# A fused decoder block on one core: low parts of 28 weight chunks are made early, kept in DRAM and loaded

## The chip, the core and the metric

The kernel runs on one core of a Trainium2 chip. Five engines each run their own instruction stream in order: TensorE (PE, matrix products into PSUM), VectorE (DVE), ScalarE (ACT), GpSimd (POOL) and SyncE (SP), which here only issues DMA transfers. GpSimd issues some transfers too. The metric is the time of one execution in device microseconds (us), the median of several runs. A run with the hardware profiler leaves a trace; its span, from the first to the last instruction, is a little shorter than the time.

## The reference

One decoder block on 512 tokens of width 1024, in fp32. The first half is token mixing: a combined input projection, a gated MLP with a causal position mixing, sliding-window attention with 16 heads, two gates, an output projection, and layer normalisation. The second half is a retrieval among 16384 single-neuron experts: each of 8 heads picks 16 experts for each token by a product of two key sets. Cut to what matters here:

```python
def peer_layer(xt, w_pq, sub_k1, sub_k2, peer_u, peer_v):
    ...
        v1, i1 = lax.top_k(s1, PEER_TOPK)
        v2, i2 = lax.top_k(s2, PEER_TOPK)
        ...
        sc, ci = lax.top_k(cand, PEER_TOPK)
        e = (...i1... * PEER_NKEYS + ...i2...)
        g = jax.nn.softmax(sc, axis=-1)
        act = gelu(jnp.einsum('thkd,td->thk', peer_u[e], xb))
        return jnp.einsum('thk,thkd->td', (g * act), peer_v[e])
```

peer_u and peer_v are matrices of 16384 rows of width 1024, called U and V below.

## The kernel before

**Split products.** A fp32 product is made as three products of a faster type: each operand is split into a high part (hi, a copy rounded by ScalarE) and a low part (lo = raw - hi, a subtraction). `mm3` (lines 62 to 64) adds hi\*hi, lo\*hi and hi\*lo in PSUM. For a chunk of weights, `load_split2` loads raw (128 x 1024, 512 KB) through SyncE's queue (L447), copies hi on ScalarE (L450) and subtracts lo, on VectorE (L458) or, in one stage, on GpSimd (L456). Four raw buffers, three hi and three lo are in turn.

**Dense experts.** For 384 of the 512 tokens the kernel doesn't gather rows: it multiplies all of them by all 16384 rows of U, in 128 chunks of 128 experts (psU, 24 matmuls of 128x384 a chunk), applies gelu, multiplies by the routing weights G and adds the products with V (acc). The last 128 tokens are done by gathers (ru, rv) that GpSimd issues, with VectorE doing the arithmetic.

**Stages.** In order of time: (1) modulation, projections and attention; 16 attention groups (4 blocks of queries x 4 groups of heads), each with its scores (pss), mask and softmax on VectorE and ScalarE (sm, ast), transposes of sm on TensorE (pt), a masked copy (pc, pp), and an output po that is split into oThi and oTlo; the products of w_gv are put between the groups to keep TensorE busy. Then w_u projections with a layer norm (vln), position mixing (pssp), gates and the output projection. (2) U chunks 3 and up beside the top-k, whose instructions a generator issues between chunks (`pump`). Their activations go to a DRAM tensor (Ad). (3) The spread: for 24 batches of 16 tokens, VectorE builds one-hot tiles oh (L633 to L637), TensorE multiplies them into a dense weight table (psg, L645 and L646), ScalarE copies that into stg (two buffers), and SyncE writes it to a DRAM tensor Gd (L658). Beside it run 28 more U chunks. Of the first 21 the activations stay in SBUF (`res`, the resident chunks; before: 32 to 52), and their part of the table is multiplied straight from stg, so it isn't written. (4) V products of the resident chunks, then U and V of the remaining ones in runs of up to 8 chunks (G is loaded from Gd by run), then V products of the spilled chunks, with Ad loaded back.

**What sets the order.** The program is written in the order in which the engines get it, with the generators' instructions put in by `pump`; a scheduler with priorities then orders each engine's stream. In SyncE's stream a transfer waits for its buffer, and all behind it wait too.

## Time and profile before

| | |
|---|---|
| time, median of 3 runs | 1730.35 us (1728.38 to 1731.13) |
| the profiled execution | 1727.13 us, span 1725.4 us |
| mean granted TensorE clock | 0.993 of full speed |
| TensorE busy | 1667.5 us, 97% of the span |
| VectorE busy | 1346.7 us, 78% |
| ScalarE busy | 685.6 us, 40% |
| GpSimd busy | 474.2 us, 27% |
| DMA | 409.52 MB, mean 237 GB/s |

A share of the whole span is a mean over stages with different limits, so the stages have to be read apart. TensorE's matmuls are pipelined and their ends are modelled: a busy TensorE is not one at its peak. An instruction is busy from its start; what it waited for stands as idle time before it.

### The profile page before, as it was taken

How to read it: one execution, taken by the hardware profiler on the slowest of the kernel's cores; microseconds unless marked ns; L12 is line 12 of the kernel's file. 1: busy time of each engine (PE TensorE's matmuls, PEld its weight loads, DVE VectorE, ACT ScalarE, POOL GpSimd, SP SyncE). 2: the span in 40 equal slices, each digit the busy share in tenths (PEclk: the TensorE clock that was granted, in tenths of full speed). 3: DMA queues.
4: the chain of work that ended last, by engine and by line, in shares of the span. 5: the costliest groups of instructions: out<-in, count | busy, mean ns of one | idle time of the engine just before them, and what ended most of it. 6: DMA issues, size and time to landing. Idle time of an engine off the chain costs nothing.

```text
span 1725.4 us, 23595 instructions
## 1 busy us (share of the span) xinstructions
PE 1667.5 (97%) x8658; PEld 1440.2 (83%) x8658; DVE 1346.7 (78%) x2510; ACT 685.6 (40%) x1095; POOL 474.2 (27%) x333
## 2 busy tenths in 40 slices
PE   6999999999999999999999999999999999999997
PEld 3865778788788999999987789999999999988776
DVE  6467785554559999999988887878787888787687
ACT  3467632233333333455443233333333333343333
POOL 2000000000043455300014544434444545541102
PEclk9999999999999999999999999999999999999999
DMA  7502267642232355566599999999899899899973
GB/s 270 200 1 74 98 198 256 210 144 95 86 120 85 112 173 174 209 218 226 203 316 365 373 328 333 325 339 348 306 336 334 326 336 341 303 372 312 306 235 106
DMA packets 158695, 409.52 MB, mean 237 GB/s; under 512 B 19217, under 2 KB 66097, under 8 KB 158322
## 3 DMA queue, kind: packets, MB, share of 16 engines
q1 hardware_dynamic: 121186, 273.47, 46.2%
q0 software_dynamic: 36960, 134.50, 21.6%
q8 instruction: 68, 1.11, 0.3%
q14 instruction: 49, 0.40, 0.1%
q10 hardware_dynamic: 432, 0.04, 0.0%
HBM read 376.88 MB, written 30.82 MB: 236 GB/s over the span
## 4 chain that ended last, share of the span: by engine, by line
PE 52%; DVE 20%; issue 5%; DMA 4%; POOL 2%; ACT 1%; SPq 0%; DVEq 0%; POOLq 0%; ACTq 0%
PE acc L802 7%; PE acc L803 7%; PE acc L799 7%; PE psU L64 6%; PE psU L62 6%; PE psU L63 6%; POOL ru L669 2%; DMA ar<-Ad 2%; DMA wa<-in_w_ada_dram 2%; DVE oh L634 1%; DVE loU L458 1%; DVE oh L637 1%; DVE oh L633 1%; DVE oh L636 1%; DVE loV L458 1%
## 5 line engine op out<-in xcount | busy, mean ns | idle before, releaser
L62 PE MATMUL psU<-h2Thi,hiU 128*128 128x384 f32 x1008 | 340.9, 338 | 5.4 <-ACT hiU L450 3.7
L64 PE MATMUL psU<-h2Thi,loU 128*128 128x384 f32 x1008 | 340.4, 338 | 3.5 <-DVE loU L458 3.4
L63 PE MATMUL psU<-h2Tlo,hiU 128*128 128x384 f32 x1008 | 339.2, 337 | 0.0
L802 PE MATMUL acc<-loV,wh 128*128 128x512 f32 x768 | 301.5, 393 | 5.5 <-DVE loV L458 5.5
L803 PE MATMUL acc<-hiV,wl 128*128 128x512 f32 x768 | 300.5, 391 | 0.3 <-DVE wl L785 0.3
L799 PE MATMUL acc<-hiV,wh 128*128 128x512 f32 x768 | 298.8, 389 | 1.7 <-ACT wh L784 1.7
L669 POOL DMA_INDIRECT ru<-in_peer_u_dram,idx x128 | 157.2, 1228 | 368.6 <-DVE ru L673 351.5
L682 POOL DMA_INDIRECT rv<-in_peer_v_dram,idx x128 | 174.1, 1360 | 248.3 <-DVE facc L688 221.4
L458 DVE TENSOR_TENSOR loV<-rawV,hiV 128x1024 fp32r<-128x1024 f32 x128 | 156.3, 1222 | 90.3 <-ACT hiV L450 90.2
L450 ACT ACTIVATE hiV<-rawV 128x1024 fp32r<-128x1024 f32 x128 | 135.1, 1056 | 224.3 <-PE psU L63 188.6
L450 ACT ACTIVATE hiU<-rawU 128x1024 fp32r<-128x1024 f32 x126 | 133.9, 1062 | 216.6 <-POOL loU L456 68.0
L62 PEld LDWEIGHTS psU<-h2Thi,hiU 128*128 128x128 f32 x1008 | 190.5, 189 | 8.8 <-ACT hiU L450 3.9
L64 PEld LDWEIGHTS psU<-h2Thi,loU 128*128 128x128 f32 x1008 | 190.3, 189 | 5.3 <-DVE loU L458 5.2
L63 PEld LDWEIGHTS psU<-h2Tlo,hiU 128*128 128x128 f32 x1008 | 190.6, 189 | 2.6
L802 PEld LDWEIGHTS acc<-loV,wh 128*128 128x128 f32 x768 | 144.1, 188 | 39.5 <-DVE loV L458 10.9
L673 DVE SCALAR_TENSOR_TENSOR ru<-ru,h2n 128x1024 f32<-128x1024 f32 x128 | 154.4, 1220 | 24.3 <-DMA ru<-in_peer_u_dram,idx 24.1
L803 PEld LDWEIGHTS acc<-hiV,wl 128*128 128x128 f32 x768 | 144.1, 188 | 30.8 <-DVE wl L785 1.0
L799 PEld LDWEIGHTS acc<-hiV,wh 128*128 128x128 f32 x768 | 144.2, 188 | 30.5 <-ACT wh L784 2.0
L688 DVE SCALAR_TENSOR_TENSOR facc<-rv,wg,facc 128x1024 f32<-128x1024 f32 x126 | 159.4, 1279 | 11.4 <-DMA rv<-in_peer_v_dram,idx 11.4
L784 ACT ACTIVATE wh<-wf 128x384 fp32r<-128x384 f32 x107 | 56.1, 525 | 182.1 <-DVE wf L780 106.2
L456 POOL TENSOR_TENSOR lopq<-rawpq,hipq 128x1024 fp32r<-128x1024 f32 x16 | 39.0, 2445 | 322.2 <-ACT hipq L450 322.2
L458 DVE TENSOR_TENSOR loU<-rawU,hiU 128x1024 fp32r<-128x1024 f32 x96 | 116.9, 1218 | 2.8 <-ACT hiU L450 2.8
(629 smaller groups left out, 2929.4 us busy)
## 6 DMA issues: line engine op xcount, KB each, us to landing
rawU<-in_uT_dram SPq DMA_DIRECT2D x128, 512.0 KB, 4.2
rawV<-in_peer_v_dram SPq DMA_DIRECT2D x128, 512.0 KB, 6.2
wa<-in_w_ada_dram SPq DMA_DIRECT2D x48, 512.0 KB, 4.2
G<-Gd SPq DMA_DIRECT2D x11, 1536.0 KB, 14.8
Gd<-stg SPq DMA_DIRECT2D x24, 600.0 KB, 4.3
rawpq<-in_w_pq_dram SPq DMA_DIRECT2D x16, 512.0 KB, 3.6
Ad<-act SPq DMA_DIRECT2D x39, 192.0 KB, 2.2
ar<-Ad SPq DMA_DIRECT2D x9, 768.0 KB, 8.5
```

The source lines that it names most:

```text
L62: nc.tensor.matmul(ps, l.hi, r.hi, start=(i == 0), stop=False)
L63: nc.tensor.matmul(ps, l.hi, r.lo, start=False, stop=False)
L64: last = nc.tensor.matmul(ps, l.lo, r.hi, start=False, stop=(i == n - 1))
L450: h = nc.scalar.activation(hi, raw, AF.Copy)
L458: last["dve"] = nc.vector.tensor_sub(lo, raw, hi.bitcast(F32))
L669: d = nc.gpsimd.indirect_dma_start(out=rows, out_offset=None, in_=I["peer_u"], in_offset=bass.IndirectOffsetOnAxis(ap=idx[:, s:s + 1], axi ...
L673: paced(nc.vector.scalar_tensor_tensor(rows, rows, 1.0, h2n, op0=ALU.mult, op1=ALU.mult, accum_out=wg[:, s:s + 1]))
L682: nc.gpsimd.indirect_dma_start(out=rows, out_offset=None, in_=I["peer_v"], in_offset=bass.IndirectOffsetOnAxis(ap=idx[:, s:s + 1], axis=0))
L688: paced(nc.vector.scalar_tensor_tensor(fa, rows, wg[:, s:s + 1], fa, op0=ALU.mult, op1=ALU.add))
L799: m = nc.tensor.matmul(acc, l.hi, r.hi, start=st, stop=False)
L802: nc.tensor.matmul(acc, l.hi, r.lo, start=False, stop=False)
L803: nc.tensor.matmul(acc, l.lo, r.hi, start=False, stop=sp_)
```

## The change

A generator `presplit` is added to the first stage. For each of the last 28 chunks of U (100 to 127) it loads raw (praw, two buffers) through GpSimd's queue, makes hi (phi) on ScalarE and lo (plo) on VectorE, one buffer each, and writes lo to a new DRAM tensor LoD, again through GpSimd's queue. It advances one step after each attention group (two after every fourth), one in each w_u projection, and what is left is issued behind the position mixing. Its loads are kept behind the second of two small transfers kd on that queue. The filling of sm with a constant, in the first four groups, goes from GpSimd to VectorE.

In the spread stage the chunks beside the spreading are now 100 to 127 (before 32 to 59), in the same number: 100 to 120 resident, 121 to 127 spilled. For them `load_split2` loads lo from LoD through SyncE in place of subtracting. Raw is loaded and hi is copied as before. The chunks that are run later with V are 32 to 99 (before 60 to 127). As the resident columns of the table stand elsewhere, the write of stg to Gd has other pieces: 128x1600 and 128x112 in place of 128x512 and 128x1200.

```diff
+NPS = 28
...
+    LoD = dram.tile([NPS, P, D], F32, name="LoD")
...
+        def presplit():
+            raws = {}
+
+            def load(k):
+                raws[k] = pre.tile([P, D], F32, name=f"praw{k}", tag="praw", bufs=2)
+                behind(nc.gpsimd.dma_start(raws[k], I["uT"][NCH - NPS + k]), kd_copy)
+            load(0)
+            for k in range(NPS):
+                if k + 1 < NPS:
+                    load(k + 1)
+                yield
+                hi = pre.tile([P, D], F32R, name=f"phi{k}", tag="phi", bufs=1)
+                lo = pre.tile([P, D], F32R, name=f"plo{k}", tag="plo", bufs=1)
+                nc.scalar.activation(hi, raws[k], AF.Copy)
+                nc.vector.tensor_sub(lo, raws[k], hi.bitcast(F32))
+                nc.gpsimd.dma_start(LoD[k], lo.bitcast(F32))
+        ps_steps = presplit()
...
             else:
-                nc.gpsimd.memset(sm, NEG)
+                nc.vector.memset(sm, NEG)
...
                 u = 4 * n + gh
+                for _ in range(2 if u % 4 == 3 else 1):
+                    next(ps_steps, None)
...
             ps = proj_T(load_split(I["w_u"][j], f"u{j}"), hT, f"psu{j}")
+            next(ps_steps, None)
...
             nc.vector.tensor_sub(aT.lo[:, g, :], mf, aT.hi[:, g, :].bitcast(F32))
+        for _ in ps_steps:
+            pass
         sp_.close()
+        pre_.close()
...
-    def load_split2(src, nm, pool=None):
+    def load_split2(src, nm, pool=None, low=None):
...
-        if last.get("pool"):
+        if low is not None:
+            nc.sync.dma_start(lo.bitcast(F32), low)
+        elif last.get("pool"):
             last["pool_lo"] = nc.gpsimd.tensor_sub(lo, raw, hi.bitcast(F32))
...
-        w = load_split2(I["uT"][i], f"U{i}")
+        w = load_split2(I["uT"][i], f"U{i}", low=LoD[i - NCH + NPS] if i >= NCH - NPS else None)
...
-        res["first"] = cur[0] + 1
+        res["first"] = NCH - NPS
...
-    i = NPRE + 1
+    todo, ready = list(range(NPRE + 1, NCH - NPS)), list(range(NCH - NPS, NCH))
     while not done or len(res["ids"]) < NRES:
-        cur[0] = i
+        i = (ready if res and ready else todo).pop(0)
...
     for _ in range(VDLY):
+        i = (ready or todo).pop(0)
         U_chunk(i, False)
...
-    uvruns = runs(range(i, NCH))
+    todo += ready
+    uvruns = runs(todo)
```

VectorE's stream where the attention groups begin, before. wloq and wwlogv are low parts of weights, sm0_0 and sm0_1 the scores of the first two groups.

```order
L120 TENSOR_TENSOR wloq7_493<-rawq7_490,whiq7_492 128x1024
L130 TENSOR_TENSOR wwlogv0_577<-rawwgv0_3_590,wwhigv0_576 128x1024
L254 COPY_PREDICATED sm0_0_543<-mcur_i_533,pss0_0_544 128x512
L258 TENSOR_REDUCE ast0_0_551<-sm0_0_543 128x4
L259 TENSOR_TENSOR ast0_0_551<-ast0_0_551,sink_538 128x4
L260 TENSOR_SCALAR ast0_0_551<-ast0_0_551 128x4
L261 TENSOR_TENSOR ast0_0_551<-sink_538,ast0_0_551 128x4
L254 COPY_PREDICATED sm0_1_594<-mcur_i_533,pss0_1_595 128x512
```

The same place now; a row with L224 is a subtraction of `presplit`.

```order
L127 TENSOR_TENSOR wloq7_497<-rawq7_494,whiq7_496 128x1024
L137 TENSOR_TENSOR wwlogv0_585<-rawwgv0_3_598,wwhigv0_584 128x1024
L224 TENSOR_TENSOR plo2_742<-praw2_640,phi2_741 128x1024
L224 TENSOR_TENSOR plo3_749<-praw3_706,phi3_748 128x1024
L283 COPY_PREDICATED sm0_0_547<-mcur_i_537,pss0_0_548 128x512
L287 TENSOR_REDUCE ast0_0_555<-sm0_0_547 128x4
L288 TENSOR_TENSOR ast0_0_555<-ast0_0_555,sink_542 128x4
L289 TENSOR_SCALAR ast0_0_555<-ast0_0_555 128x4
L290 TENSOR_TENSOR ast0_0_555<-sink_542,ast0_0_555 128x4
L283 COPY_PREDICATED sm0_1_602<-mcur_i_537,pss0_1_603 128x512
L287 TENSOR_REDUCE ast0_1_610<-sm0_1_602 128x4
L224 TENSOR_TENSOR plo4_819<-praw4_746,phi4_818 128x1024
```

Two subtractions, plo2 and plo3, stand between the last weights and the first masking (COPY_PREDICATED), and plo4 stands inside the second group's softmax.

GpSimd's stream behind the two kd transfers, now (before, two fillings of sm, MEMSET, and the masking of wst followed there).

```order
L236 DMA kd1_386<-kd1_386 64x512
L215 DMA praw0_580<-in_uT_dram 128x1024
L215 DMA praw1_582<-in_uT_dram 128x1024
L225 DMA LoD_79<-plo0_636 128x1024
L215 DMA praw2_640<-in_uT_dram 128x1024
L225 DMA LoD_79<-plo1_702 128x1024
L215 DMA praw3_706<-in_uT_dram 128x1024
L225 DMA LoD_79<-plo2_742 128x1024
```

Each load praw stands ahead of the store LoD of the chunk before; a store waits for its subtraction, and the next load waits behind it.

SyncE's stream in the middle of the spread, before: the writes of the table by batch (stg0_2 is batch 2 of the first 128 tokens), and the raw chunks.

```order
L658 DMA Gd_76<-stg0_2_6217 128x512
L658 DMA Gd_76<-stg0_2_6217 128x1200
L658 DMA Gd_76<-stg0_3_6304 128x512
L658 DMA Gd_76<-stg0_3_6304 128x1200
L447 DMA rawU41_6793<-in_uT_dram 128x1024
L658 DMA Gd_76<-stg0_4_6391 128x512
L658 DMA Gd_76<-stg0_4_6391 128x1200
L447 DMA rawU42_6880<-in_uT_dram 128x1024
```

Now:

```order
L690 DMA Gd_76<-stg0_2_6418 128x1600
L690 DMA Gd_76<-stg0_2_6418 128x112
L486 DMA loU106_6732<-LoD_79 128x1024
L690 DMA Gd_76<-stg0_3_6505 128x1600
L690 DMA Gd_76<-stg0_3_6505 128x112
L486 DMA loU107_6819<-LoD_79 128x1024
L477 DMA rawU110_7081<-in_uT_dram 128x1024
L690 DMA Gd_76<-stg0_4_6592 128x1600
```

A load loU stands between the writes of two batches, behind the write of an earlier one, and the loads rawU run four chunks ahead of it.

And SyncE's stream at the end of the spread, now.

```order
L690 DMA Gd_76<-stg2_6_8205 128x1600
L690 DMA Gd_76<-stg2_6_8205 128x112
L486 DMA loU125_8363<-LoD_79 128x1024
L750 DMA Ad_77<-act124_8287 128x384
L477 DMA rawU126_8396<-in_uT_dram 128x1024
L690 DMA Gd_76<-stg2_7_8290 128x1600
L690 DMA Gd_76<-stg2_7_8290 128x112
L486 DMA loU126_8399<-LoD_79 128x1024
L750 DMA Ad_77<-act125_8391 128x384
L477 DMA rawU127_8432<-in_uT_dram 128x1024
L486 DMA loU127_8435<-LoD_79 128x1024
L477 DMA rawV100_8468<-in_peer_v_dram 128x1024
```

Chunk 127's raw stands behind the write of chunk 125's activations (act125), and the loads of the last two low parts stand just ahead of and behind it.

## Rows read from the trace of the kernel before

**Rows 1.** The page, busy time, share of the span and instructions of each engine.

```profile
PE 1667.5 (97%) x8658; PEld 1440.2 (83%) x8658; DVE 1346.7 (78%) x2510; ACT 685.6 (40%) x1095; POOL 474.2 (27%) x333
```

**Rows 2.** Table by stages: length, busy us (instructions), granted clock, DMA share, GB/s.

```profile
84.00:196.00 112.00, 110.92 (x530) 70.96 (x530) 73.06 (x179) 75.32 (x207) 1.05 (x2) 1.00 0.09 29
196.00:231.00 35.00, 34.76 (x154) 28.42 (x153) 29.83 (x42) 21.12 (x25) 1.59 (x1) 1.00 0.64 218
231.00:260.00 29.00, 24.32 (x139) 20.76 (x137) 28.12 (x43) 11.65 (x16) 0.00 (x0) 0.98 0.57 192
...
713.00:890.00 177.00, 169.18 (x1443) 162.79 (x1444) 170.86 (x207) 91.43 (x180) 3.80 (x3) 0.97 0.68 236
890.00:1000.00 110.00, 102.91 (x456) 83.65 (x455) 90.04 (x134) 35.86 (x47) 54.03 (x44) 1.00 0.99 364
1000.00:1500.00 500.00, 500.00 (x2531) 455.38 (x2530) 403.22 (x499) 182.11 (x241) 229.33 (x174) 1.00 0.93 330
```

**Rows 3.** TensorE's timeline, 713 to 891 us: start, length, operation, idle before.

```profile
713.15 0.45 PE L617 MATMUL ptg<-ident,gs 128*128 128x128 f32 x1 [2.32 <-DVE gs L597]
...
723.96 0.24 PE L645 MATMUL psg<-oh,oh 128*128 128x128 f16 x1
...
725.76 0.22 PE L646 MATMUL psg<-oh,oh 128*128 128x128 f16 x1
...
882.68 0.33 PE L64 MATMUL psU<-h2Thi,loU 128*128 128x384 f32 x1
...
889.96 0.33 PE L64 MATMUL psU<-h2Thi,loU 128*128 128x384 f32 x1
890.14 0.39 PE L799 MATMUL acc<-hiV,wh 128*128 128x512 f32 x1
```

**Rows 4.** VectorE's groups, 713 to 890 us: count, busy us, mean ns, idle before.

```profile
L458 DVE TENSOR_TENSOR loU<-rawU,hiU 128x1024 fp32r<-128x1024 f32 x26 | 31.6, 1215 | 2.3 <-ACT hiU L450 2.3
L636 DVE TENSOR_TENSOR oh<-oh,gT 128x2048 f16<-128x2048 f16 x24 | 29.1, 1214 | 0.1
```

**Rows 5.** DMA issues of the whole run: count, KB each, median us to landing.

```profile
rawU<-in_uT_dram SPq DMA_DIRECT2D x128, 512.0 KB, 4.2
...
rawpq<-in_w_pq_dram SPq DMA_DIRECT2D x16, 512.0 KB, 3.6
Ad<-act SPq DMA_DIRECT2D x39, 192.0 KB, 2.2
...
ru<-in_peer_u_dram,idx POOLq DMA_INDIRECT x128, 7.4
```

**Rows 6.** Waits of SyncE's DMA queue, 700 to 930 us: total, times, longest.

```profile
SPq L447 <- DVE loU L458: 68.9, 21, 8.2
```

**Rows 7.** The page, costliest groups: count, busy us, mean ns, idle before.

```profile
L669 POOL DMA_INDIRECT ru<-in_peer_u_dram,idx x128 | 157.2, 1228 | 368.6 <-DVE ru L673 351.5
...
L450 ACT ACTIVATE hiU<-rawU 128x1024 fp32r<-128x1024 f32 x126 | 133.9, 1062 | 216.6 <-POOL loU L456 68.0
```

**Rows 8.** GpSimd's timeline, 30 to 90 us.

```profile
58.72 0.57 POOL L207 DMA_DIRECT2D kd<-kd  x1
```

**Rows 9.** DMA issues between 50 and 80 us.

```profile
kd<-kd POOLq DMA_DIRECT2D x2, 128.0 KB, 2.5
```

**Rows 10.** VectorE's timeline, 72 to 93 and 194 to 198 us.

```profile
84.40 0.73 DVE L254 COPY_PREDICATED sm<-mcur_i,pss 128x512 f32<-128x512 int32 x1 [7.84 <-PE pss L249]
...
196.08 0.43 DVE L288 TENSOR_TENSOR oTlo<-po,oThi 128x256 fp32r<-128x256 f32 x1 [0.43 <-ACT oThi L287]
```

**Rows 11.** TensorE's timeline, 81 to 93 us.

```profile
90.48 0.60 PE L271 MATMUL pt<-ident,sm 128*128 128x128 f32 x4
```

**Rows 12.** VectorE's groups, 84 to 196 us.

```profile
L274 DVE TENSOR_TENSOR pc<-pt,mcurT 128x512 f32<-128x512 f32 x16 | 11.0, 687 | 5.9 <-PE pt L271 5.8
...
L288 DVE TENSOR_TENSOR oTlo<-po,oThi 128x256 fp32r<-128x256 f32 x15 | 6.4, 423 | 14.8 <-ACT oThi L287 14.7
...
L259 DVE TENSOR_TENSOR ast<-ast,sink 128x4 f32<-128x4 f32 x16 | 2.5, 155 | 0.1
```

More of the change, by code (lines that the diff above doesn't have):

```diff
@@ L65, in mm3, with behind @@
         return last
+    def behind(ins, other):
+        tc.add_manual_dep(ins.ins, other.ins.name,
+                          mybir.DependencyInfo(mybir.DependencyClass.NoSync, mybir.DependencyReason.DATA))
     const = ctx.enter_context(tc.tile_pool(name="const", bufs=1, reuse_waits="tile"))
@@ L197, in block_kernel @@
                 nc.tensor.matmul(ps, w.lo[:, k, :], hT.hi[:, k, :], start=False, stop=(k == NK - 1))
+        pre_ = ExitStack()
+        pre = pre_.enter_context(tc.tile_pool(name="pre", bufs=1, reuse_waits="tile"))
+        def presplit():
[14 more added lines that the diff above has]
+        ps_steps = presplit()
         att = ExitStack()
@@ L206, in block_kernel @@
         nc.gpsimd.dma_start(kd[0][64:128, :], kd[0][0:64, :])
-        nc.gpsimd.dma_start(kd[1][0:64, :], kd[1][64:128, :])
+        kd_copy = nc.gpsimd.dma_start(kd[1][0:64, :], kd[1][64:128, :])
         vT = ap_.tile([P, S], F32, name="vT", tag="pc", bufs=2)
@@ L435, in block_kernel @@
     last = {}
-    def behind(ins, other):
-        tc.add_manual_dep(ins.ins, other.ins.name,
-                          mybir.DependencyInfo(mybir.DependencyClass.NoSync, mybir.DependencyReason.DATA))
     def paced(ins):
         behind(ins, last["dve"])
-    def load_split2(src, nm, pool=None):
+    def load_split2(src, nm, pool=None, low=None):
         raw = pw.tile([P, NK * P], F32, name=f"raw{nm}", tag="raw", bufs=4)
@@ L710, in U_chunk @@
     def U_chunk(i, keep_act):
-        w = load_split2(I["uT"][i], f"U{i}")
+        w = load_split2(I["uT"][i], f"U{i}", low=LoD[i - NCH + NPS] if i >= NCH - NPS else None)
         ps = pu.tile([P, SD], F32, name=f"psU{i}", tag="mm", bufs=2)
@@ L816, in block_kernel @@
     res = {}
-    cur = [NPRE]
     def end_topk():
@@ L867, in block_kernel @@
             pump(GPUMP if res else UPUMP + 1.2 * bool(last.get("pool")))
-        i += 1
     open_v()
     for _ in range(VDLY):
+        i = (ready or todo).pop(0)
         U_chunk(i, False)
@@ L873, in block_kernel @@
         pump(2.7)
-        i += 1
-    uvruns = runs(range(i, NCH))
+    todo += ready
+    uvruns = runs(todo)
     for n, j in enumerate(res["ids"]):
@@ L899, in block_kernel @@
     left = 260 - n_g
-    for run in runs(spilled):
+    for run in runs(sorted(spilled)):
         load_G(run)
```

## The prediction

> **What bounds the kernel now.** The share of busy time says TensorE, 97% of the span [rows 1]. That is an average, so I cut the span into stages [rows 2]. Three of them are touched.
>
> The spread stage runs from its first transpose at 713.15 to the first product with V at 890.14, 177.0 us [rows 3]. VectorE is busy 170.86 of the 177 there [rows 2], and the groups show with what: 24 batches, each with four builds of 1.21 us, and 26 subtractions loU of 1.215 us, 31.6 us together [rows 4]. TensorE's 169.18 looks nearly full, but its records overlap and stretch when it is fed late, so I count its own need from step lengths. psU matmuls follow each other every (889.96 - 882.68)/42 = 0.1733 us, psg matmuls every (725.76 - 723.96)/31 = 0.0581 us [rows 3]. By program order there are 668 psU and 768 psg matmuls between those two ends: 115.8 + 44.6 = 160.4 us. The 48 changes between the two shapes and the nine transposes have no row of their own; I put them at 3.6, a little above one psg step each: 164.0 (without them 160.4). So TensorE loses 13.0 us here, and that is the most that freeing VectorE can return; the 31.6 us are not.
>
> The attention stage, 84 to 196 us, is the opposite: TensorE 110.92 of 112.00, VectorE 73.06, ScalarE 75.32, DMA share 0.09 [rows 2]. Work put on VectorE has room, but a TensorE instruction that waits for it costs its full wait. In the next stage (196 to 231) VectorE has 29.83 of 35, and from 231 to 260 it is full, 28.12 of 29 [rows 2].
>
> The third is the entrance to V, 890 to 1000: DMA share 0.99, 364 GB/s, and TensorE 102.91 of 110 [rows 2]. There bytes are the price.
>
> **The spread.** 26 to 28 loU subtractions leave VectorE: 31.6 us, and up to 34. Its 170.86 falls to about 138 of 164, and TensorE's 164 becomes the bound. In their place come as many loads loU of 512 KB. In the order SyncE issues them behind the Gd write of an earlier batch, and their buffer (three) is free when TensorE has finished the chunk three before. I followed the order: most are asked for 12 to 15 us before use, and a load of 512 KB lands in 4.2 us [rows 5]. DMA: before, 236 GB/s x 177 us = 41.8 MB; 24 more loads are 12.6 MB, 54.4 MB in 164 us, 331 GB/s. From 1000 to 1500 DMA carries 330 GB/s at a share of 0.93 with TensorE at 500.00 of 500 [rows 2], so this is at the edge but carried. A wait that goes: rawU's buffer was freed by the subtraction, and SyncE waited 68.9 us in all for it [rows 6]; now ScalarE's copy frees it. Where it ends is less good. The last three chunks (125 to 127) have rawU and loU issued behind writes of act, with leads of 3.5 to 7.7 us against 4.2 of landing; VectorE would have needed 1.2 us there. I leave 3.5 us of TensorE's wait in place. Value 13.0 - 3.5 = **-9.5 us**; bounds 0 (every load as late as the subtraction was) and -13.0.
>
> The Gd writes change from 128x512 + 128x1200 to 128x1600 + 128x112, the same bytes, 448 B a row in the small one. Two staging buffers cover a batch of some 7 us each, and a write of 600 KB should land near rawU's 4.2 for 512 KB [rows 5]: nothing, unless it passes some 12 us.
>
> **The front.** 28 subtractions of 1.22 us and 28 copies on ScalarE of 1.06 us [rows 7] come here. In the attention stage 17 of them: VectorE 73 + 20.7 + four moved memsets, some 95 of 112; ScalarE 75 + 18 = 93 of 112. By busy time they fit. What may not fit is the wait. plo has one buffer: subtraction k+1 can't write before the store LoD of k has landed, and VectorE is in order, so everything behind it waits for that round trip r. No row shows a 512 KB store from POOL's queue. Its parts: the issue on POOL took 0.57 us for kd and 1.23 us for ru [rows 7, 8]; the landing of kd, 128 KB on that queue, 2.5 us, of Ad (192 KB, to DRAM) 2.2, of rawpq (512 KB) 3.6 [rows 5, 9]. From Ad to rawpq 320 KB cost 1.4 us, so 384 KB more than kd cost 1.7: 2.5 + 1.7 = 4.2, and I take r = **4.3** from the subtraction's end; bounds 3.6 (a landing like rawpq's, its issue hidden) and 7.4 (the median of the gathers ru on that queue [rows 5]).
>
> By program order plo2 and plo3 stand back to back ahead of the first masking. Before, VectorE idled 7.84 us until 84.40 [rows 10]; I put plo1's end at 74.2, plo2's at max(79, 78.5) + 1.2 = 80.2, plo3's at 80.2 + 4.3 + 1.2 = 85.7. The first masking begins 1.3 us late, and plo4 follows inside the second group: it starts at 85.7 + 4.3 = 90.0, after which the first group's sm is done at 92.9, where TensorE had used it at 90.48 [rows 11]: 2.4 us lost at once. Group four, with small pieces around its subtraction, I put at 1.6 more: **+4**.
>
> After that, between plo3 and plo19, the order has 16 pieces of VectorE work. With mean durations by shape (0.69, 0.42 and 0.16 us [rows 12], 1.22 for 128x1024) they are 3.3, 4.3, 3.5, 5.6, 3.4, 6.5, 2.7, 12.9, 4.1, 3.9, 4.4, 4.4, 4.2, 4.9, 4.2 and 4.2 us. A step is the larger of its piece and r, and 1.22. With r = 4.3 the sum is 81.7 + 19.5 = 101.2, plo19 ends at 186.9, and the last oTlo 4.9 us later at 191.8, ahead of the 196.08 of before [rows 10]. So only the early stalls stay. With r = 5.0 it is 90.0 + 19.5 from 86.4: 195.9, last oTlo 200.8, +4.7; beyond that each 0.1 us of r costs 1.3 us: +8.6 at 5.3, +11 at 5.5, +18 at 6. The front is thus **+4**, bounds +1 (r = 3.6) and, at 7.4, more than 30.
>
> Behind attention 11 subtractions are left for 196 to 260: 8 of them beside the w_u projections, where VectorE has 5 us free and gets 10 more of work, part of which moves into the full 29 us; it ends at a wait of TensorE that the +4 already contains if VectorE arrives early. I add nothing, and up to 3 for the range.
>
> DMA pays nothing here: 0.09 of it was used in attention, and 17 x 1.05 MB in 112 us are 160 GB/s.
>
> **A rule that speaks against it.** On POOL's queue the trace shows the ru issue at 1228 ns against 570 for kd [rows 7, 8], both beside a working VectorE. The Trainium skill, "SBUF — State Buffer", section "Who interferes with whom", says that descriptors of DMAs issued from GpSimd can't be written while VectorE runs a copy, cast or tensor_scalar in a two-port mode, and that tensor_tensor doesn't hinder it. In the attention stage nearly all of VectorE's work is tensor_tensor, reduce or masked copy, so by that rule r would stay as short as I take it; with the gap of 0.66 us between the two issues added to each trip r would be 5.0 and the front +4.7 or a little more. The same skill, "DMA: Bandwidth & Descriptors", section "Anatomy of one DMA — SWDGE (gpsimd) path", warns that the completion of a write into HBM can take surprisingly long; Ad's 2.2 us into DRAM [rows 5] doesn't show that on SyncE's queue, and no run here shows it on POOL's.
>
> **The entrance to V.** Three chunks' loU (125 to 127) fall on or next to the stage where DMA is full: 1.57 MB / 364 GB/s = 4.3 us if all of it delays the V loads; most of it is asked for before 890. Value **+1**, bounds 0 and +4.3. The chunks later read in runs are 32 to 99 instead of 60 to 127, 68 both times, the spilled ones 39 both times: nothing.
>
> **Sum.** -9.5 + 4 + 1 = -4.5 us. The profiled execution took 1727.13 us, 3.2 below the median of 1730.35; to that median the forecast is **1725.9 us**.
>
> **The rivals.** *A, the forecast*: spread -7 to -13, front +1 to +5: 1717 to 1726.8. *M, the front takes it back*: r of 5.0 to 5.4, front +5 to +10 and a little in the stages behind; with -9.5 and +1 the sum is -3.5 to +3.4, 1729 at its middle. For it: one buffer, 17 trips, and no slack in TensorE; against it: Ad's short landing. *B, slower, the LoD round trip*: the same place, but decided from r = 5.5 on, where the front's loss passes 12 us: r of 5.5 to 6 gives +3.5 to +10, 1734 to 1740. For it: the gathers' 7.4 on the same queue; against it: those are indirect. *C, slower, the loads pace the spread*: SyncE's one queue carries rawU, loU, Gd and Ad in order, a Gd write waits for ScalarE's stg, and a loU behind it is late; it decides when the lead of 12 to 15 us falls below the landing, which at 297 GB/s or more (331 asked) may grow. Then the stage keeps its 177 us and the front's +4 and the +1 remain: 1735. For it: the 0.99 share behind 890 with TensorE losing 7 us [rows 2]; against it: 1000 to 1500.
>
> **How the numbers follow.** About 0.2% (3.5 us) is what a measurement of this kernel can tell from no change. A 0.45, M 0.27, B 0.16, C 0.12. So faster 0.45, same 0.27, slower 0.28. The range takes A's better end and most of B and C: 1716 to 1739; A alone would be 1717 to 1727.
>
> **What would show it.** Right: loU gone from VectorE between 713 and 890, that stage near 167 us with VectorE near 140, no long TensorE wait for a loU load before chunk 125; in the front each plo waiting about a trip behind the one before, the first group's transposes of sm some 2 us later, the last oTlo before 197. Wrong: LoD landing above 5 us after its subtraction (then M or B, with VectorE's waits named LoD from 84 to 196 and the last oTlo past 200), or psU idle behind DMA loU in many chunks of the spread (C). If the spread gains more than 13 us, my step lengths are wrong.

## The result and the profile after

The changed kernel is slower: 1741.01 us median (1738.57 to 1743.42) against 1729.37 for the kernel before on the same chip, a ratio of 1.0066 with a 95% interval of 1.0049 to 1.0084. The profiled execution took 1740.37 us, span 1738.6, mean granted clock 0.987.

Busy times, the page's first part, for [rows 1]: VectorE has as much work as before, only elsewhere; ScalarE has 27 us more and GpSimd 34.

```profile
PE 1668.6 (96%) x8658; PEld 1439.3 (83%) x8658; DVE 1348.4 (78%) x2514; ACT 712.8 (41%) x1123; POOL 508.2 (29%) x385
```

The table by stages, for [rows 2], with the spread stage (727 to 897) and the entrance to V (897 to 1007) where they now lie; columns as there.

```profile
84.00:196.00 112.00, 105.30 (x512) 68.03 (x511) 86.57 (x191) 89.06 (x221) 17.03 (x32) 0.95 0.56 190
196.00:231.00 35.00, 30.34 (x124) 22.36 (x123) 29.09 (x41) 20.64 (x25) 6.45 (x11) 0.90 0.73 256
...
727.00:897.00 170.00, 166.18 (x1453) 160.20 (x1451) 142.93 (x180) 93.72 (x183) 4.55 (x4) 1.00 0.88 320
897.00:1007.00 110.00, 104.28 (x447) 83.66 (x447) 91.82 (x136) 35.87 (x48) 56.83 (x44) 0.98 1.00 370
```

TensorE lost 5.6 us of busy time in attention and 4.4 in the stage behind it, and its clock fell to means of 0.95 and 0.90 where it had been 1.00. In the spread it is the other way round: VectorE has 142.93 of 170, and TensorE has 166.18 at a clock of 1.00, where the mean clock was 0.97.

By the same instruction in both traces: the first gate product (psgb) starts 12.8 us later (232.86, now 245.70), the first U matmul 16.8 (471.17, 487.93), the first transpose of the spread 17.7 (709.51, 727.24), the first product with V 6.6 (890.14 [rows 3], 896.76), the last one 9.2 (1714.84, 1723.99). TensorE's rows, before:

```profile
471.17 0.44 PE L62 MATMUL psU<-h2Thi,whiU 128*128 128x384 f32 x1 [1.79 <-ACT h2Thi L428]
709.51 0.27 PE L617 MATMUL ptg<-ident,i1s 128*128 128x128 f32 x1
1714.84 0.39 PE L803 MATMUL acc<-hiV,wl 128*128 128x512 f32 x1
```

and after:

```profile
487.93 0.44 PE L63 MATMUL psU<-h2Thi,whiU 128*128 128x384 f32 x1 [1.79 <-ACT h2Thi L463]
727.24 0.27 PE L649 MATMUL ptg<-ident,i1s 128*128 128x128 f32 x1
728.79 0.30 PE L649 MATMUL ptg<-ident,gs 128*128 128x128 f32 x1 [0.46 <-DVE gs L629]
896.76 0.40 PE L831 MATMUL acc<-hiV,wh 128*128 128x512 f32 x1
1723.99 0.39 PE L835 MATMUL acc<-hiV,wl 128*128 128x512 f32 x1
```

So the front lost 17.7, the spread gave back 11.1, V lost 2.5, and 4.0 more were lost behind the last product: 13.1 of the 13.2 us between the profiled executions. The start that the prediction took for the spread, 713.15, is that of the third transpose (of gs), now 728.79; by that end the front lost 15.6 and the spread gave back 9.0 (177.0, now 168.0).

What the spread gave back. Before, TensorE's waits there sum to 9.6 us, and at the two longest (2.32 us until 713.15, 3.69 until 874.68) and behind them the granted clock stood near 0.50, that is 1.2 GHz in place of 2.4:

```profile
713.00:716.40 3.40, 3.25 (x11) 3.28 (x12) 3.40 (x5) 0.55 (x2) 2.78 (x2) 0.50 1.03 393
873.30:880.10 6.80, 5.17 (x15) 4.66 (x16) 5.67 (x6) 3.77 (x6) 0.00 (x0) 0.51 0.75 261
```

Half of the two lengths is 5.1 us, an estimate of what they cost. Now the waits are 3.4 us, and no stretch is below full clock. 6.2 us of waits and 5.1 of clock are about the 11.1 us (some 0.8 is counted twice, as the stretches begin within the waits).

Where the front's loss starts. VectorE's timeline (start, length, operation, idle before, and for what), at two places, and between them the last oTlo, which ends attention:

```profile
80.82 1.22 DVE L224 TENSOR_TENSOR plo<-praw,phi 128x1024 fp32r<-128x1024 f32 x1
87.62 1.23 DVE L224 TENSOR_TENSOR plo<-praw,phi 128x1024 fp32r<-128x1024 f32 x1 [5.59 <-DMA LoD<-plo]
88.77 0.72 DVE L283 COPY_PREDICATED sm<-mcur_i,pss 128x512 f32<-128x512 int32 x1
...
204.51 0.42 DVE L317 TENSOR_TENSOR oTlo<-po,oThi 128x256 fp32r<-128x256 f32 x1 [0.18 <-ACT oThi L316]
...
214.79 1.23 DVE L224 TENSOR_TENSOR plo<-praw,phi 128x1024 fp32r<-128x1024 f32 x1 [3.65 <-DMA LoD<-plo]
```

ScalarE's, just behind the second place:

```profile
216.10 1.06 ACT L223 ACTIVATE phi<-praw 128x1024 fp32r<-128x1024 f32 x1 [3.17 <-DVE plo L224]
217.06 1.04 ACT L126 ACTIVATE whiu<-rawu 128x1024 fp32r<-128x1024 f32 x1
```

And what TensorE made of both (at the first place, scores wait until the masking has read their buffer):

```profile
89.54 0.80 PE L278 MATMUL pss<-kd,qT 64*128 64x128 f32 x4 [2.59 <-DVE sm L283]
...
218.16 0.50 PE L63 MATMUL psu<-hThi,whiu 128*128 128x512 f32 x1 [3.66 <-ACT whiu L126]
```

The second place is the one to read. A subtraction waits for the store before it; the next copy phi stands on ScalarE behind that subtraction; the rounded weight whiu of a projection stands on ScalarE behind phi; and TensorE waits for whiu. No instruction in this chain took long. The round trip from a subtraction's end was 5.6 us at the first place (82.0 to 87.62) and 8.1 at the second (206.7, the end of the one before, to 214.79).

A wait costs more than itself. The same view by short stretches, where the granted clock stood at 0.50:

```profile
89.60:93.00 3.40, 3.40 (x13) 2.69 (x14) 2.69 (x7) 3.37 (x10) 0.61 (x2) 0.50 0.63 214
134.00:140.80 6.80, 6.30 (x19) 3.25 (x20) 5.33 (x9) 4.98 (x8) 0.00 (x0) 0.50 0.36 114
219.30:226.10 6.80, 5.80 (x15) 4.52 (x15) 6.80 (x9) 4.28 (x6) 1.07 (x2) 0.50 0.73 243
```

Each follows a wait of TensorE: of 2.59 us that ended at 89.54, 1.95 at 133.09, 3.66 at 218.16. At half speed each gives up half of its length, 1.7 or 3.4 us, at most. Before, there was one such stretch in the front, from 259.0, at the one long wait there. Up to the first gate product TensorE's waits sum to 11.4 us against 1.1, and the half-speed stretches cost 8.5 against 0 by that estimate; that is more than the delay of 12.8, since some later products were also moved ahead (the first pssp now starts 27.0 us before that gate product, before 1.7).

### The profile page after: what moved, and what is told of

The parts are those of the page before. It is cut to its first block, busy times and chain, and to the rows that moved or that the text cites. A ratio compares the mean times of both kernels' runs of the same rounds, so it can differ in the third digit from the quotient of the medians.

```text
span 1738.6 us, 23813 instructions
## 1 busy us (share of the span) xinstructions
PE 1668.6 (96%) x8658; PEld 1439.3 (83%) x8658; DVE 1348.4 (78%) x2514; ACT 712.8 (41%) x1123; POOL 508.2 (29%) x385
## 4 chain that ended last, share of the span: by engine, by line
PE 69%; issue 11%; DMA 8%; DVE 7%; POOL 4%; ACT 1%; SPq 0%; DVEq 0%; POOLq 0%; ACTq 0%
PE psU L65 9%; PE psU L63 9%; PE psU L64 9%; PE acc L834 7%; PE acc L835 7%; PE acc L831 7%; DMA ar<-Ad 3%; DMA wa<-in_w_ada_dram 3%; POOL ru L701 2%; PE psq L63 2%; PE psq L65 2%; PE psq L64 2%; PE psg L677 1%; DVE loV L490 1%; PE psg L678 1%
## 5 line engine op out<-in xcount | busy, mean ns | idle before, releaser
L714 POOL DMA_INDIRECT rv<-in_peer_v_dram,idx x128 | 177.9, 1390 | 245.6 <-DVE facc L720 223.9
L488 POOL TENSOR_TENSOR loU<-rawU,hiU 128x1024 fp32r<-128x1024 f32 x30 | 74.9, 2497 | 59.3 <-ACT hiU L480 59.3
```

Source lines behind the costliest of these rows:

```text
L714: nc.gpsimd.indirect_dma_start(out=rows, out_offset=None, in_=I["peer_v"], in_offset=bass.IndirectOffsetOnAxis(ap=idx[:, s:s + 1], axis=0))
```

## The experiments

Two theories stood at the start. **W**: the early work costs by its waits, VectorE and ScalarE standing in order at transfers. **P**: it costs by the place of its 28 copies and 28 subtractions in those two streams. A third, **C**, was that the transfers slow other loads. In the tables "first U" is the start of the first psU matmul in the profiled execution (before: 471.2) and "spread" the time from its first transpose to the first product with V (before: 180.6).

### The two halves of the change apart

`e1_subtract_again`:

```diff
-        w = load_split2(I["uT"][i], f"U{i}", low=LoD[i - NCH + NPS] if i >= NCH - NPS else None)
+        w = load_split2(I["uT"][i], f"U{i}")
```

> The low parts are made and stored early as in the changed kernel, but beside the spreading VectorE subtracts them once more and LoD is never read. Theory (the early work costs about 17 us up to the first U chunk, the spread returns about 11): all of the cost and none of the gain, 1729.4 + 17 + 4 at the end of the program = about 1750 us, 1746 to 1752. Rival (the changed order of chunks or the loads cost it, not the early work): near 1729 to 1735.

`e2_no_front`:

```diff
-            for k in range(NPS):
-                if k + 1 < NPS:
+            for k in range(1):
+                if k + 1 < 1:
...
-        w = load_split2(I["uT"][i], f"U{i}", low=LoD[i - NCH + NPS] if i >= NCH - NPS else None)
+        w = load_split2(I["uT"][i], f"U{i}", low=LoD[0] if i >= NCH - NPS else None)
```

> Only one low part is made early; all 28 chunks beside the spreading load that one (their low parts are therefore false). Theory: the spread's gain alone, about 11 us, less 2.5 us in V: 1721 us if the 4 us at the end of the program come with the transfers on GpSimd's queue, 1725 if they come with the loads. The first U matmul starts within 1 us of its start before. Rival (the delay in the front is not the presplit's): 1735 or more.

| | median us | ratio to before (95%) | first U | spread |
|---|---|---|---|---|
| subtract again | 1748.27 | 1.0102 (1.0079 to 1.0125) | 484.1 | 181.4 |
| no front | 1726.74 | 0.9974 (0.9959 to 0.9990) | 475.7 | 169.0 |

Both halves are real: early work without the loads loses 17.8 us, loads without the early work gain 3.7, which makes +14.1, where the whole change has +11.6. The spread is 11.6 us shorter with loads and as long as before without: where VectorE subtracts again, TensorE's waits there (9.8 us) and two half-speed stretches (5.1 us) are back. Its front is that of the changed kernel, and its trace has the time from issue to landing of the 28 stores LoD, and the median of the 17 in attention (84 to 196 us):

```profile
DMA to landing us min/median/max: 2.9/3.2/8.6
...
LoD<-plo POOLq DMA_DIRECT2D x17, 512.0 KB, 3.0
```

The second one's table by stages, its spread stage:

```profile
715.00:884.00 169.00, 165.57 (x1451) 159.96 (x1450) 142.26 (x180) 93.45 (x183) 4.44 (x4) 1.00 0.88 320
```

Its median lies 1.7 and 5.7 us above my two values, and its first U matmul is 4.5 us late where I expected at most 1. In its profiled execution a stretch at half clock follows a wait of 1.57 us at 127.39; the kernel of the transfers alone (below) has the same wait of 1.57 at 126.80 and no such stretch. So not every wait is followed by one, and executions of one kernel differ: 1721.34 to 1731.65 us here.

### Which wait it is

`e3_no_store` leaves 27 of the 28 stores out:

```diff
-                nc.gpsimd.dma_start(LoD[k], lo.bitcast(F32))
+                if k == 0:
+                    nc.gpsimd.dma_start(LoD[k], lo.bitcast(F32))
```

(and all chunks load LoD[0].)

> All 28 copies and subtractions stay in the front, but only the first low part is stored and all chunks load that one (low parts false). Theory 1 (the round trip of the store with one buffer plo holds VectorE and, behind it, ScalarE and TensorE): about 13 of the 17 us go, 1728 us, or 1724 if the 4 us at the end go with the stores. Theory 2 (the copies and subtractions stand in the way by their own place in ScalarE's and VectorE's order, or wait for praw): the front stays 14 us or more late, 1738 to 1741.

`e4_in_place` has two shared tiles for hi and lo, in the same space:

```diff
-                hi = pre.tile([P, D], F32R, name=f"phi{k}", tag="phi", bufs=1)
-                lo = pre.tile([P, D], F32R, name=f"plo{k}", tag="plo", bufs=1)
+                hi = pre.tile([P, D], F32R, name=f"phi{k}", tag="phi", bufs=2)
...
-                nc.vector.tensor_sub(lo, raws[k], hi.bitcast(F32))
-                nc.gpsimd.dma_start(LoD[k], lo.bitcast(F32))
+                nc.vector.tensor_sub(hi, raws[k], hi.bitcast(F32))
+                nc.gpsimd.dma_start(LoD[k], hi.bitcast(F32))
```

> The result is the full one; hi and lo share one tile, of which there are two, so a subtraction no longer waits for the store just before it but the copy waits for the store two before. Theory 1: the round trip of 5.6 us is hidden by two steps of 6 us or more, and the front falls from 17 to about 4 us: 1728 to 1731 us. Theory 2: nothing of note, 1738 to 1742.

`e5_no_transfers` does all copies and subtractions on one raw chunk:

```diff
-                if k + 1 < NPS:
-                    load(k + 1)
...
-                nc.scalar.activation(hi, raws[k], AF.Copy)
-                nc.vector.tensor_sub(lo, raws[k], hi.bitcast(F32))
-                nc.gpsimd.dma_start(LoD[k], lo.bitcast(F32))
+                nc.scalar.activation(hi, raws[0], AF.Copy)
+                nc.vector.tensor_sub(lo, raws[0], hi.bitcast(F32))
+                if k == 0:
+                    nc.gpsimd.dma_start(LoD[k], lo.bitcast(F32))
```

> The 28 copies and subtractions stay in the front, all on the one raw chunk loaded first, and only the first result is stored; all 28 chunks load that one (low parts false). So neither copy nor subtraction waits for a transfer. Theory W (in the front VectorE and ScalarE, in order, stand at waits for the transfers praw and LoD): TensorE's wait of 2 to 5 us near 90 us goes, the first U matmul is at most 5 us later than before, and the time is that of the kernel without the early work, 1726 to 1729 us. Theory P (the 28 + 28 instructions themselves stand ahead of the softmax in the two streams): the front stays 8 us or more late, 1733 to 1737.

`e6_transfers_alone` moves everything and computes nothing:

```diff
+    RaD = dram.tile([NPS, P, D], F32, name="RaD")
...
+                if k > 0:
+                    nc.gpsimd.dma_start(RaD[k], raws[k])
+                    continue
```

> All 28 loads and 28 stores on GpSimd's queue stay, but after the first step raw is stored to another tensor and no copy or subtraction is made; all chunks load the first low part (low parts false). Theory W or P: moving 29 MB beside the front costs TensorE nothing there, so the time is that of the kernel without the early work plus the 4 us at the end of the program, 1729 to 1732 us. Theory C (the transfers slow the weight loads of the front): TensorE waits for weights between 60 and 260 us, 1734 us or more.

| | median us | ratio to before (95%) | first U |
|---|---|---|---|
| no store | 1736.57 | 1.0035 (1.0022 to 1.0048) | 479.2 |
| two tiles, in place | 1736.32 | 1.0041 (1.0029 to 1.0054) | 478.6 |
| no transfers | 1718.10 | 0.9930 (0.9911 to 0.9949) | 465.7 |
| transfers alone | 1729.98 | 1.0001 (0.9984 to 1.0017) | 472.6 |

The first two came out between the values forecast for them. The two last settle it for W in attention. All of the work without the transfers costs nothing, and the time is below both values forecast: VectorE goes from 73.06 to 88.57 us there, ScalarE from 75.32 to 90.83 [rows 2], and TensorE keeps 110.24 of 112. No transfers, 84 to 196:

```profile
84.00:196.00 112.00, 110.24 (x548) 72.09 (x548) 88.57 (x195) 90.83 (x224) 0.00 (x0) 1.00 0.10 34
```

All of the transfers without the work cost TensorE nothing either, at a DMA share of 0.71. Transfers alone, 84 to 196, and the last store on GpSimd's queue:

```profile
84.00:196.00 112.00, 110.34 (x530) 70.45 (x529) 74.18 (x181) 75.11 (x207) 25.35 (x47) 1.00 0.71 255
...
183.61 0.54 POOL L223 DMA_DIRECT2D RaD<-praw  x1 [2.04 <-DMA praw<-in_uT_dram]
```

With that store the transfers were over before the stage behind attention began, so this run can't rule out C there. The load of wst, the weights of the position mixing, which GpSimd then masks, landed in 7.1 us before:

```profile
wst<-in_w_sp_dram SPq DMA_DIRECT2D x1, 512.0 KB, 7.1
```

With two tiles, beside loads and stores of the low parts, it took 12.0, and TensorE waited for the masking:

```profile
wst<-in_w_sp_dram SPq DMA_DIRECT2D x1, 512.0 KB, 12.0
...
223.56 0.91 PE L360 MATMUL pssp<-wst,vln 128*128 128x128 f32 x4 [3.85 <-POOL wst L344]
```

In the changed kernel GpSimd began that masking 7.8 us after the load was issued, no wait of TensorE is named after it, and from 60 to 290 us ScalarE waited 4.9 us for loads of weights (before 4.6). So C has a part in such versions, behind attention, and hardly one in the change itself.

That the kernel with no transfers is even 8.6 us faster than the one with no front I put down to the order: up to the first U matmul, TensorE's waits and half-speed stretches cost 8.6 us in the one profiled execution and 15.3 in the other, in orders that differ. In attention only the two together cost. P and C are out as whole explanations. But my first form of W, that it is the store's round trip with one buffer, is only half of it: without stores the front is still 8 us late. There the raw loads are the late ones. No store, ScalarE's timeline ahead of the first masking:

```profile
82.27 1.06 ACT L223 ACTIVATE phi<-praw 128x1024 fp32r<-128x1024 f32 x1 [2.12 <-DMA praw<-in_uT_dram]
86.13 1.06 ACT L223 ACTIVATE phi<-praw 128x1024 fp32r<-128x1024 f32 x1 [2.80 <-DMA praw<-in_uT_dram]
```

and VectorE's:

```profile
83.36 1.23 DVE L224 TENSOR_TENSOR plo<-praw,phi 128x1024 fp32r<-128x1024 f32 x1 [2.44 <-ACT phi L223]
87.22 1.23 DVE L224 TENSOR_TENSOR plo<-praw,phi 128x1024 fp32r<-128x1024 f32 x1 [2.63 <-ACT phi L223]
88.36 0.72 DVE L284 COPY_PREDICATED sm<-mcur_i,pss 128x512 f32<-128x512 int32 x1
```

The mask that the first softmax needs stands behind three subtractions, each behind a copy, each behind a load. Take one wait away, and the next one holds the same two streams.

### Holding the work back, and half of it

`e9_all_held` (with the two tiles) holds each copy behind the exponentials and each subtraction behind the scaling of its attention group. `e8_half_held` does that for every second low part; beside the spreading the other 14 are subtracted.

```diff
-                nc.scalar.activation(hi, raws[k], AF.Copy)
-                nc.vector.tensor_sub(lo, raws[k], hi.bitcast(F32))
-                nc.gpsimd.dma_start(LoD[k], lo.bitcast(F32))
+                behind(nc.scalar.activation(hi, raws[k], AF.Copy), held["act"])
+                behind(nc.vector.tensor_sub(hi, raws[k], hi.bitcast(F32)), held["dve"])
+                nc.gpsimd.dma_start(LoD[k], hi.bitcast(F32))
```

The half version also has

```diff
-                for _ in range(2 if u % 4 == 3 else 1):
+                for _ in range(1 if u > 0 else 0):
...
-        w = load_split2(I["uT"][i], f"U{i}", low=LoD[i - NCH + NPS] if i >= NCH - NPS else None)
+        w = load_split2(I["uT"][i], f"U{i}", low=LoD[(i - NCH + NPS) // 2] if i >= NCH - NPS and i % 2 == 0 else None)
```

> The result is the full one. Only every second of the 28 low parts is made early, copy and subtraction are held behind the exponentials and the scaling of their attention group, and hi and lo share a tile of which there are two. The 14 subtractions left beside the spreading are 17 us; with 14 away VectorE's work there is 171 - 17 = 154 us, under TensorE's 164, so nearly the whole gain should stay (8 to 11 us). Front: no wait of TensorE near 90 us, at most 3 us late. End of the program +2 us. 1723 to 1727 us by both W and P. If the spread's gain halves, 1728 to 1731.

> The result is the full one. All 28 low parts, held and in shared tiles as in the half version. Theory P: the order is what cost, and the front is 3 to 6 us late: 1728 to 1733 us with the 4 us at the end. Theory W: with two tiles and the same transfers the front gains only what sharing the tiles gave, 1734 to 1738.

`e10_half_first_held` is the half version with only the first copy and subtraction held (`if k == 0`); `e13_all_first_held` is that with all 28; `e14_half_free` is the half version with none held.

> The result is the full one. As the half version, but only the first copy and subtraction are held behind the first attention group; the others go where the order puts them. Theory W: the waits depend on how long before its use a load was issued, so little changes against the half version held throughout: 1726 to 1730 us. If holding each of them was itself a cost, 1722 to 1726.

> The result is the full one. All 28 low parts in shared tiles as in the kernel with two tiles (1736 us), but with the first copy and subtraction held behind the first attention group. If the three or more early subtractions ahead of the first softmax are the cost: TensorE's wait of 5 us near 93 us goes, the first U matmul is within 4 us of before, 1722 to 1728 us with the 4 us at the end. If the number of early low parts is the cost: 1732 to 1737.

> The result is the full one. Every second low part, in shared tiles, nothing held: six subtractions stand ahead of the first masking. If their place is the cost: TensorE waits 3 to 8 us near 90 us for the mask, 1722 to 1729 us, at least 6 us over the version with the first one held (1716.5). If only the number counts: within 3 us of 1716.5.

| | median us | ratio to before (95%) | first U | spread |
|---|---|---|---|---|
| half, each held | 1728.40 | 0.9981 (0.9968 to 0.9993) | 477.1 | 173.2 |
| all, each held | 1761.28 | 1.0170 (1.0145 to 1.0194) | 506.2 | 170.8 |
| half, first held | 1716.50 | 0.9900 (0.9880 to 0.9921) | 464.6 | 171.0 |
| half, none held | 1720.78 | 0.9937 (0.9920 to 0.9954) | 469.6 | 171.5 |
| all, first held | 1741.85 | 1.0064 (1.0048 to 1.0081) | 484.5 | 169.4 |

Only the half version with each held came out at a value forecast for it, and not for the reason given there: its spread gained 7.4 us, and its first U matmul was 5.9 late. The others missed all of theirs. Half of the low parts give the spread nearly all that 28 give (9.6 of 11.1 us), since VectorE only has to fall below TensorE. In the half version with none held, the wait for the first mask is there, longer than in the changed kernel, since the copy ahead of it waits 7.55 us for its raw load:

```profile
94.53 0.81 PE L277 MATMUL pss<-kd,qT 64*128 64x128 f32 x4 [5.58 <-DVE sm L282]
```

and it is about what lies between 1720.78 and 1716.50 (4.3 us; 5.0 between the first U matmuls). But with all 28 the same hold is no help, it loses some 5 us (1736.32, then 1741.85), and holding all of them loses 25. My expectation that the place ahead of the first softmax was the whole cost is wrong; going from 14 to 28 costs 16 us with none held and 25 with the first held. All held, ScalarE's waits from 60 to 290 us (total, times, longest) and the stage 240 to 290:

```profile
ACT phi L224 <- DMA praw<-in_uT_dram: 18.4, 8, 5.7
```

```profile
240.00:290.00 50.00, 37.78 (x155) 30.88 (x156) 42.33 (x58) 22.83 (x29) 6.41 (x12) 0.80 0.62 219
```

What is held back in attention comes later, into the stage of the w_u projections.

### Number or place

`e15_half_behind_attention` makes the same 14 in the w_u loop, held behind the last attention group. `e16_twenty` makes 20 of the 28 within the attention groups and none behind, the first held.

```diff
-                for _ in range(2 if u % 4 == 3 else 1):
-                    next(ps_steps, None)
...
-            next(ps_steps, None)
+            for _ in range(2):
+                next(ps_steps, None)
```

```diff
+    sel = [i for i in range(NCH - NPS, NCH) if (i - NCH + NPS) % 7 not in (3, 6)]
...
+        next(ps_steps)
         for n in range(NT):
```

> The result is the full one. The same 14 low parts as in the best version, but all of them behind the attention groups, beside the w_u projections, where before 64% of DMA and 38 of 44 us of VectorE were taken. If the place is the cost (steps there wait for transfers on a busy DMA and hold the layer norm and the weights' halves): TensorE loses 8 us or more between 196 and 260 us, 1726 to 1736 us. If only the number counts: 1715 to 1721 us.

> The result is the full one. 20 of the 28 low parts, all within the attention groups, none behind them; the first held as in the best version. If the place is the cost: near the best version, 1714 to 1721 us (a little less left to subtract beside the spreading, 0.4 us more at the end). If the number is: 1723 to 1732 us.

| | median us | ratio to before (95%) | first U | spread |
|---|---|---|---|---|
| 14 behind attention | 1736.52 | 1.0043 (1.0024 to 1.0062) | 487.2 | 171.0 |
| 20 within attention | 1722.09 | 0.9950 (0.9934 to 0.9965) | 467.6 | 170.5 |

The same 14 low parts cost 20 us more behind attention than within it; 20 within it cost 5.6 more than 14, of which 1.0 behind the last product, and their 1722.09 lies between the two values forecast. It is mostly the place. The 14 behind attention, 196 to 240, and one of TensorE's waits there:

```profile
196.00:240.00 44.00, 38.06 (x157) 28.82 (x156) 35.67 (x46) 23.89 (x29) 10.96 (x18) 0.92 0.88 313
```

```profile
216.38 0.68 PE L361 MATMUL pssp<-wst,vln 128*128 128x128 f32 x4 [2.48 <-DVE vln L356]
```

The 20 within it:

```profile
84.00:196.00 112.00, 111.17 (x528) 71.65 (x528) 88.14 (x187) 85.16 (x209) 19.18 (x36) 1.00 0.58 202
196.00:240.00 44.00, 41.64 (x191) 31.29 (x190) 40.32 (x61) 26.01 (x43) 2.17 (x3) 0.96 0.58 197
```

In attention DMA had a share of 0.09 and VectorE 39 us to spare; from 196 on DMA was at 0.64 and VectorE had 5 [rows 2]. In the first place a load is early and a wait has slack around it, in the second neither. The 14 stores landed in 3.0 us (median) within attention and in 4.4 behind it, and wst, 6.6 us beside the first, took 11.2 beside the second.

### GpSimd in their stead

`e11_gpsimd_subtracts` (two tiles, all 28) has `nc.gpsimd.tensor_sub`; `e12_gpsimd_alone` has `nc.gpsimd.tensor_copy` for the copy as well.

> The result is the full one. All 28 low parts; GpSimd subtracts (2.45 us each) in place of VectorE, ScalarE still copies, hi and lo share a tile of which there are two. Theory W: VectorE no longer waits for praw or LoD, but ScalarE does; the wait of TensorE near 90 us goes, 1730 to 1735 us. If ScalarE's waits are the whole cost: 1736 or more. If GpSimd's subtractions slow VectorE's attention work beside them: VectorE's busy time there rises, and the time is over 1740.

> All 28 low parts; GpSimd copies and subtracts, so that neither VectorE nor ScalarE has any of the early work (the high part is rounded by GpSimd there). Theory W: nothing that TensorE waits for stands behind a transfer, and the time is that of the transfers alone, 1728 to 1731 us: the spread's gain less the end of the program. If GpSimd's work slows VectorE or its stores come too late for the gates' tiles: over 1735.

1744.83 us (1.0066, 1.0046 to 1.0086) and 1771.46 us (1.0211, 1.0183 to 1.0239). Both miss W's numbers and lie where I had put them if GpSimd slows VectorE. That cost, which W doesn't contain, is there: some of VectorE's own instructions became longer. It isn't the only one: in the first, ScalarE's copies also waited 27.0 us for praw, and no run parts the two. GpSimd subtracts, VectorE's groups from 84 to 196 us:

```profile
L288 DVE TENSOR_SCALAR ast<-ast 128x4 f32<-128x4 f32 x12 | 10.9, 909 | 0.2
...
L287 DVE TENSOR_TENSOR ast<-ast,sink 128x4 f32<-128x4 f32 x13 | 8.7, 665 | 0.1
L302 DVE TENSOR_TENSOR pc<-pt,mcurT 128x512 f32<-128x512 f32 x12 | 8.2, 687 | 1.7 <-PE pt L299 1.6
```

GpSimd alone, the same view:

```profile
L137 DVE TENSOR_TENSOR wwlogv<-rawwgv,wwhigv 128x1024 fp32r<-128x1024 f32 x5 | 10.3, 2058 | 1.3 <-ACT wwhigv L136 1.3
```

A mean of 665 ns where it was 155 for the same tiny instruction, 2058 where it was 1219 for the split of a weight, and 687 unchanged for the product that reads one operand from PSUM [rows 12]. The Trainium skill, "SBUF — State Buffer", section "Who interferes with whom", says that a VectorE instruction with both inputs in SBUF contends with a GpSimd instruction that reads SBUF; the trace agrees, with those three means. The tensor_scalar, 909 ns where it was 163, reads only one tensor, so that sentence doesn't cover it.

### The version that beats both

Half of the low parts, in shared tiles, within attention, the first held: 1716.50 us, 0.9900 of before. Its stages:

```profile
84.00:196.00 112.00, 109.77 (x530) 70.61 (x529) 86.85 (x192) 87.00 (x220) 13.86 (x26) 1.00 0.43 155
...
240.00:290.00 50.00, 50.00 (x238) 41.78 (x237) 41.16 (x61) 15.85 (x20) 0.00 (x0) 1.00 0.73 248
704.00:875.00 171.00, 165.79 (x1450) 159.97 (x1449) 159.94 (x197) 94.29 (x183) 6.35 (x5) 1.00 0.79 279
```

The spread gives 9.6 us; V and the end of the program take 5.9 back. Another 6.6 are won in the front, which I put down to the order and not to the low parts as such: in the new order TensorE has no long wait between 240 and 290 us, where the kernel before waited 3.40 us until 259.84 and, from the end of that wait on, ran this stretch:

```profile
259.00:265.80 6.80, 5.96 (x14) 4.71 (x15) 4.31 (x7) 1.26 (x3) 0.00 (x0) 0.50 0.91 302
```

3.4 and half of the 6.0 us behind the wait are 6.4. No run moves this order alone.

## Why the prediction was wrong

It gave 1725.9 us (1716 to 1739) and 0.28 for slower; it came to 1741. By its steps:

- **The spread, -9.5.** Right: -9.0 by the prediction's own ends, -11.1 from the first transpose on. TensorE's own need was the bound, VectorE fell to 142.93 (about 138 was forecast), and C didn't come. What stayed is 3.4 us of TensorE's waits, 2.7 of them for loU loads, where I had left 3.5 us. I hadn't seen that some 5 of the 13.0 us to be won were, by the estimate above, half-speed stretches; they went with the waits.
- **The front, +4.** This step failed: +17.7 (+15.6 by the prediction's ends). Attention ended 8.4 us late (the last oTlo started at 196.08, now at 204.51, past the 200 that I had named as a sign of being wrong), and as much again was lost from there to the first U matmul. It has three errors. First the round trip: I took 4.3 us for every step, put together from other landings. It isn't one number. With the same front (subtract again) a store landed in 3.0 us in the median of attention, and in up to 8.6 outside it. Most trips were shorter than 4.3; the ones that cost were longer, 5.6 ahead of the first masking and 8.1 behind attention. Between 84 and 196 VectorE waited for a store only twice, 5.59 and 0.75 us. Rival B, with 0.16, named the store and nearly the time, but its mechanism, a trip of 5.5 us or more that paces VectorE through all of attention, didn't come; that 1734 to 1740 lies next to 1741 is largely luck. Second, that chain followed VectorE's subtractions alone. The copy on ScalarE stands in order too, and behind it the weights' copies and the exponentials; with the stores gone, the waits of copies for raw loads still made the front 8 us late. Third, the sentence on the stage behind attention: "I add nothing, and up to 3 for the range". The last subtractions fell there, beside a DMA share of 0.64 and a VectorE with 5 us free, and 14 of them alone, put there, made TensorE's first U matmul 16.0 us late.
- **The issue on GpSimd.** The issue of kd at 58.72 didn't stand beside a working VectorE, as I had read: VectorE idled for 6.22 us until 60.85. But the gap of 0.66 us between the two issues, which would have made r 5.0, didn't come: GpSimd issued each of the 28 stores in 0.54 to 0.56 us, one of them at 206.96 beside VectorE's layer-norm statistics.
- **The price of a wait.** I counted a TensorE wait at its length. Here waits were followed by stretches at a granted clock of 0.50, which by the estimate above cost 8.5 us up to the first gate product, not far below the waits' 11.4.
- **"DMA pays nothing here".** Right for TensorE in attention (the transfers alone cost it nothing), wrong as an argument that they are free: what they cost is the wait of whoever uses them.
- **The bounds of A.** Its terms, -7 to -13, +1 to +5 and +1, give 1719 to 1729, and not 1717 to 1726.8.
- **The entrance to V, +1.** +2.5, within its bounds.
- **The end.** Not in the sum: +4.0, below.
- **A Gd write in other pieces** at nothing: no wait of TensorE in the spread is named after it.

## What to carry to other kernels

Work moved into the idle time of in-order engines is free only if its inputs have landed when its turn comes. For each moved instruction ask which transfer it waits for, on a queue and in a stage how busy, and what stands behind it on its engine; the sum of its durations is the smaller question. Then ask how much has to be moved: here the second engine only had to fall below the bound, half of the moves did that, and the other half found no good place.

## What the hardware showed that I had not expected

**The end of the program grows with the plain transfers that GpSimd issues.** VectorE's last instructions, before:

```profile
1720.77 1.40 DVE L738 SCALAR_TENSOR_TENSOR xhat<-xhat,rso,fr 128x512 f32<-128x512 f32 x2
```

and after:

```profile
1729.93 1.40 DVE L770 SCALAR_TENSOR_TENSOR xhat<-xhat,rso,fr 128x512 f32<-128x512 f32 x2
```

From their end to the end of the span are 3.2 us before (1725.4) and 7.3 after (1738.6), with 56 more transfers on GpSimd's queue. With 2 more (no front) it was 3.2, with 28 (half, first held) 4.9, with 29 (no store) 5.1, with 40 (twenty) 5.9, with 56 and no early work behind them (transfers alone) 7.5: 0.06 to 0.08 us for each. The 256 gathers that GpSimd also issues are in the 3.2. What runs in that time isn't named by any row, and no run has the same transfers on another queue.

**Half clock after a wait isn't sure to come.** The wait of 1.57 us near 127 us was followed by 6.8 us at 0.50 in one kernel's profiled execution and by nothing in another's; the executions of the first (no front) lay between 1721.34 us, at a mean granted clock of 0.994, and 1731.65, at 0.989.
